# Split weights of an input projection kept in device memory by the first block and loaded by the later ones

## The chip, the cores and the metric

The kernel runs on one core of a Trainium2 chip, as one launch. The metric is device time in microseconds (us), the median of several runs. Lower is better.

## The reference

The program is one layer of a sequence model on x of 2048 tokens by 1024 channels, float32. The normalised input goes through one wide input projection; three groups of heads (a gated DeltaNet, an RWKV-7 and an HGRN2 group, 8 heads of 64 each) work on slices of it, each with a recurrence over time; their outputs go through one output projection and are added to x, and a last RMSNorm follows.

```python
def reference(x, norm_w, w_in, ...):
    for l in range(DEPTH):                      # DEPTH = 1
        h = _rmsnorm(x, norm_w[l])              # (1, 2048, 1024)
        proj = (h @ w_in[l]).astype(F32)        # the input projection
        p_gdn, p_rwkv, p_hgrn = _split(proj, (GDN_PROJ, RWKV_PROJ, HGRN_PROJ))
        y_a = _gdn_branch(p_gdn, ...)
        y_b = _rwkv7_branch(p_rwkv, ...)
        y_c = _hgrn2_branch(p_hgrn, ...)
        y = jnp.concatenate([y_a, y_b, y_c], axis=-1).astype(x.dtype)
        x = x + y @ w_out[l]
    return _rmsnorm(x, final_norm_w)
```

## The kernel before, in words

**Blocks.** The 2048 tokens go through in four blocks of 512 (`TB`, `NT` = 4). For each block, `block` (line 606) loads x, normalises it, transposes it on TensorE and leaves the normalised input in two halves of lower precision, `hhi` and `hlo`, whose sum is the value. Each block then needs the whole input projection: 49 column tiles of 128 columns, each over the 1024 input channels. A tile comes in four parts (`KD // KH`), each of 256 input channels (`KH` = 2 times 128).

**A part of a tile.** The weights are split in two as well. `fetch` (line 499) loads 128 KB of raw weights of `w_in` into a tile `wr` by a DMA on SP's queue; `split` (line 505) makes the high half `wh` by a copy on ScalarE, which rounds to the type fp32r, and the low half `wl` by a subtraction on GpSimd. The part is then six matmuls into one PSUM bank: for each of the two slices of 128 channels wh with hhi, wh with hlo, and wl with hhi. The pool `wp` has `AHEAD` = 4 buffers for wh and for wl each, and `NWR` = 3 for wr (lines 331 to 335). The names in the trace are formed from the part and the tile: wh0hg is the high half of part 0 of tile hg, wl1rv the low half of part 1 of tile rv, mmhg the PSUM bank of tile hg.

**Halves.** Five of the 49 tiles of a block, the first two (wa, rr) and the last three (rg, gg, hg of the last group of heads), are not done over the 512 tokens at once: first the first 256 tokens of each, then the second 256. These take their weights twice and their matmuls have 256 columns; their names end in h0 and h1 (the trace writes mmgg_3h). So a block has 54 tiles in the program, 216 parts.

**Prefetch.** `stream` (line 513) holds the list of parts and gives `more` (line 517): one call splits the oldest raw part, if three are loaded, and then loads the next raw part. `projections` (line 524) calls it nine times ahead and once behind the last matmul of each part (line 604), so four parts lie split and three raw ones are loaded or on their way. The output projection's first half (`first_half`, whose stream is at line 1182) uses the same `stream` and the same buffers for its activations, which it splits in the same way, toward the end of the program.

```python
                for i in range(KD // KH):
                    wh, wl = ahead.pop(0)
                    for j in range(KH):
                        k = KH * i + j
                        mm(po, wh[:, j, :], hhi[:, hs, k, :], start=(k == 0), stop=False)
                        mm(po, wh[:, j, :], hlo[:, hs, k, :], start=False, stop=False)
                        mm(po, wl[:, j, :], hhi[:, hs, k, :], start=False, stop=(k == KD - 1))
...
                    more()
```

**What else runs.** Beside the projection run the groups of heads, as threads of small operations on all engines: `block` and `decays` for a block, and for each of four pairs of heads p the threads `inputs`, `solve`, `chain`, `gates_out`, `outs` and `hgrn` (threads at line 1485). The recurrences are chains of small matmuls with VectorE in between: `S<-pc,S` adds the bank pc to the state S of the DeltaNet, `h_S<-h_S,tot` scales and adds the HGRN2 state, `g_p` is a run of 21 matmuls of 32 by 64. Loads of x (tiles xt, xa) and stores of the finished y tiles go by DMA, on SP's and ScalarE's queues.

**What sets the order.** Two things. `drive` (line 282) takes the next step of a thread by a string of letters, `ORDER` (line 84): this fixes the program. Then `lay_down` (line 269) takes a table for each of the five engines, `LANES` (lines 131 to 250), that says in which order this engine is to work off its instructions, and pins that order. `Lane` (line 253) records each instruction as it is issued, so all instructions carry line 263 in the profile; they are told apart by their tiles. The buffer pools stay as the program has them: which buffer a tile gets is set by the program, and the table of an engine can only move an instruction within what the buffers allow.

**The end.** After the last block, the second half of the output projection runs from line 1506 on (whi, wlo, yt, yh, yl), with the last RMSNorm.

Of the kernel before, what the change touches and what calls it, by code (L numbers as in the profile page):

```python
# [20 lines left out]
D = 1024  # L21
# [4 lines left out]
C = 32  # L26
# [22 lines left out]
def consts():  # L49
# [20 lines left out]
    for i, l in enumerate(LEVELS):  # L70
# [62 lines left out]
        "c-oa%eQ*`k6+ioS-@bjxOY(dnF%ZxtFDCM(5k>7t?JL1BAwY=W7dj4Y92l(QXw^<@Eq~aN5w%!sYqesF(<v6~P(`euFr~FKXjO`WPW_H8MG&Ka"  # L133
        "4T``!{oQl#-rX1NOgovq`*ru;bI$MM-WQ@%=u@ttBV0`<&@n!Z-r}kB8edAEbCw$DAm=GV%pToDTlq6Sm+Gkp{W5e0)#B}BdKHJdug4fQbQs6G"
        "G>4n<eH$&J0kl1|k-tS-xQpJ#T~VH?wn*)m?N0g?FT~h0@T>|mw_&~p`Ujs$Y5e_-&!!i-p4!l}o<`uwhkO>j%u{gn0-~8o%g`2R3O&kSqfzu1"
        "F3}KT9^y&(VjN<sMSca0`6;LI{U*$N9c|{Bc=80#!;ByD82W@8$)gDplNvii&+&9RfEhE$t&t{4HF~LwZsz4wP3w6j-OV>rKlSnkx`bcE^Sh{("
        "e#|#u)az*z&qX#H_&b!NNBA<-rUCJ8<xYB#*Q4*9bOYZ@%eftq@8RuyDqV^3nrR~4K;P#Ux`rO+D`+jNh{}8kA{mMA2arnx?GvO1QJ)sf&__@4"
        "97H+Db!b1v+&|^fG!K<tPOEu|#9u=-Xh#6WI{Hk|s-nEKFC(Td<kLw{Vy+_cS<U@GO5rvGM=M<_H7TOctKdc&_!cnQK1BW=>fL}$XQ9Ryqt@^6"
        "5YNXr(^1o1h)#`PM`cuf6t2sNTE#vZy>mFK=qL{LHb5I-W}lAp+Zeas#@$5I!H^%JI(^{9BvMg-h-efRAD|-RX+PQn==W869jM;R<ZR>xyq(TR"
        "rF&7CPPz*0%FxX~p#yAez#K*T9^HW$zD*DCAfEtUOrSS0Z!Jc7hL0nnHdOBviE9j<N_%+}eZ=QTtm9CPxv0Tf+;@OARft+~-xY<Z>n!@6i2m(3"  # L140
        "PLyw|rR|qGE<$dLkjD<N`Y;gQj4D6Rdr`kVm}@cKT#Nd>#<$Y#INm`N{{jYkI7GgqQFo=dv%%2GQo+1nyInBs5q9;{g<wNJ@Om1!6j6a$$YrJ="
        "Swvn>^KAKM2k<$95w*&8K~dYm`gag@8W^>JC8O~43TWyqe7BA-f*x9Er0BI9RVtzq$M`6?aEyDQZdJoF5YpJz(;;X^Il)5IxFNyDD#OMqWU?DR"
        "^D=)$W{$GS(`}MRC)z$}|3;kGKw}eVIpR>-`#E0?oiT6X9%$=0?}UaUKT%8$=p|GrO|$6_yq`}-HdlZpe}V=#0J$Df<D=kW3-Egs${GZ3&j(h`"
        "sB9CCR#dzLY?_EK$Dj_?w99CsOQKhCW)S`Rh&)4oHSw!lXQDRk;(@OS);;2v>jd$!(8;yd6?%b08)99?KR~1p^EVLfcM(M|W$7opkrwkl@M}EY"
# [148 lines left out]
def kernel_body(ctx, tc, x, w_in, w_ba, w_lora, w_out, fnw, lnw, par, kst, msk, out, T, dbg=None):  # L293
# [45 lines left out]
    with ExitStack() as ph:  # L339
# [173 lines left out]
        def stream(parts):  # L513
# [1100 lines left out]
```

## Time and profile before

| | us |
|---|---|
| median of 3 runs | 2440.32 |
| the three runs | 2442.41, 2440.32, 2426.66 |
| the profiled execution | 2438.88 |
| its span (first to last instruction) | 2436.9 |
| mean granted clock of TensorE in the span | 0.967 |

The profile is of one execution on the chip. The engines are PE (TensorE matmul), PEld (TensorE's weight loads, which overlap PE), DVE (VectorE), ACT (ScalarE), POOL (GpSimd) and SP, which only issues DMAs here. The granted clock (PEclk) is the share of full speed that the throttle gave TensorE. A view of waits names an engine's first instruction after idle time, and with an arrow what ended it; "issue" means that the profile shows nothing that the engine waited for. In names of tiles the numbers of the block and of the group of heads are mostly left out.

### The profile page before, as it was taken

How to read it: one execution, taken by the hardware profiler on the slowest of the kernel's cores; microseconds unless marked ns; L12 is line 12 of the kernel's file. 1: busy time of each engine (PE TensorE's matmuls, PEld its weight loads, DVE VectorE, ACT ScalarE, POOL GpSimd, SP SyncE). 2: the span in 40 equal slices, each digit the busy share in tenths (PEclk: the TensorE clock that was granted, in tenths of full speed). 3: DMA queues.
4: the chain of work that ended last, by engine and by line, in shares of the span. 5: the costliest groups of instructions: out<-in, count | busy, mean ns of one | idle time of the engine just before them, and what ended most of it. 6: DMA issues, size and time to landing. Idle time of an engine off the chain costs nothing.

```text
span 2436.9 us, 88807 instructions
## 1 busy us (share of the span) xinstructions
PE 2233.4 (92%) x38264; PEld 1771.3 (73%) x38264; DVE 1625.5 (67%) x3430; ACT 1024.0 (42%) x2234; POOL 1203.4 (49%) x1641
## 2 busy tenths in 40 slices
PE   6999999989999999899999999888989998899898
PEld 5777676777777777777777778766777777676687
DVE  4867676767676777777676678666675767641354
ACT  5444444445444444454434445444434443422332
POOL 4655455555445555655555455544455644554200
PEclk8999999989999999999999999899999999899999
DMA  3212122221212122222121121212121112446764
GB/s 111 75 53 73 50 69 72 77 79 61 71 46 75 48 75 66 95 65 73 52 70 56 57 77 63 84 54 66 51 67 58 63 61 71 140 143 211 233 214 170
DMA packets 208153, 206.94 MB, mean 85 GB/s; under 512 B 19472, under 2 KB 179600, under 8 KB 207760
## 3 DMA queue, kind: packets, MB, share of 16 engines
q1 hardware_dynamic: 194944, 173.48, 22.3%
q10 hardware_dynamic: 12816, 27.79, 3.3%
q8 instruction: 299, 4.90, 0.8%
q14 instruction: 94, 0.77, 0.1%
HBM read 171.84 MB, written 29.36 MB: 83 GB/s over the span
## 4 chain that ended last, share of the span: by engine, by line
PE 60%; DVE 26%; issue 5%; DMA 3%; POOL 3%; ACT 2%; SPq 0%; ACTq 0%; POOLq 0%; DVEq 0%
PE pa L263 5%; PE mmrk L263 4%; PE pc L263 4%; PE mmgq L263 3%; PE mmgv L263 3%; PE mmhf L263 3%; PE mmhq L263 3%; DVE slv L263 3%; DVE Tf L263 3%; PE mmrr L263 3%; PE uW L263 2%; DVE h_S L263 2%; DMA wry<-ydram 2%; PE mmgk L263 2%; PE g_p L263 2%
## 5 line engine op out<-in xcount | busy, mean ns | idle before, releaser
L263 PEld LDWEIGHTS pc<-S,M 128*128 128x128 f32 x1024 | 144.9, 193 | 48.1 <-DVE S L263 19.1
L263 PE MATMUL pc<-S,M 128*128 128x64 f32 x1024 | 153.9, 273 | 15.5 <-DVE S L263 9.8
L263 POOL TENSOR_TENSOR wly<-wry,why 128x256 fp32r<-128x256 f32 x96 | 70.8, 746 | 91.4 <-ACT why L263 88.0
L263 DVE TENSOR_TENSOR S<-pc,S 128x128 f32<-128x128 f32 x256 | 72.9, 285 | 63.2 <-PE pc L263 61.6
L263 DVE SCALAR_TENSOR_TENSOR h_S<-h_S,tot 128x64 f32<-128x64 f32 x256 | 100.8, 394 | 17.9 <-ACT h_S L263 13.4
L263 DVE TENSOR_TENSOR slv<-Af,Tf 128x15 f32<-128x15 f32 (+7 forms) x240 | 82.4, 343 | 6.1
L263 DVE TENSOR_TENSOR Tf<-Tf,slv 128x15 f32<-128x15 f32 (+7 forms) x240 | 81.5, 340 | 6.3
L263 ACT ACTIVATE why<-wry 128x256 fp32r<-128x256 f32 x96 | 39.4, 416 | 105.4 <-DMA wry<-ydram 53.4
L263 POOL TENSOR_TENSOR D<-gw,cst 128x512 f32<-128x512 f32 x64 | 70.9, 1112 | 23.3 <-DVE M L263 9.2
L263 POOL TENSOR_TENSOR ss<-ss,mhalf 128x1 f32<-128x1 f32 x16 | 8.8, 550 | 131.7 <-DVE ss L263 131.7
L263 PEld LDWEIGHTS h_l<-h_q,h_k 64*32 64x32 f32 x4096 | 41.5, 107 | 29.2 <-DVE h_P L263 12.3
L263 DVE TENSOR_TENSOR h_k<-h_k,tot 128x256 f32<-128x256 f32 x64 | 37.4, 584 | 31.3 <-PE h_l L263 31.3
L263 PE MATMUL h_l<-h_q,h_k 64*32 64x32 f32 x4096 | 48.7, 201 | 7.5 <-DVE h_P L263 5.5
L263 DVE TENSOR_TENSOR M<-MA,D 64x512 f32<-64x512 f32 x64 | 43.9, 686 | 16.1 <-PE MB L263 14.0
L263 PE MATMUL pa<-whi,yl 128*128 128x512 f32 x128 | 50.9, 397 | 2.5 <-DVE yl L263 2.5
L263 PE MATMUL pa<-whi,yh 128*128 128x512 f32 x128 | 50.6, 395 | 0.0
L263 ACT ACTIVATE uW<-uW 128x1024 f32<-128x1024 f32 x32 | 32.8, 1024 | 42.0 <-PE uW L263 42.0
L263 PE MATMUL pa<-wlo,yh 128*128 128x512 f32 x128 | 50.4, 394 | 0.0
L263 POOL TENSOR_TENSOR h_e<-h_k,h_q 128x512 f32<-128x512 f32 (+1 forms) x32 | 37.6, 1175 | 24.5 <-DVE h_q L263 23.9
L263 DVE TENSOR_TENSOR h_q<-h_q,tot 128x256 f32<-128x256 f32 x64 | 39.1, 611 | 15.7 <-PE h_l L263 15.7
L263 DVE COPY_PREDICATED h_P<-mlev,h_l 128x128 f32<-128x128 int32 x128 | 36.6, 294 | 18.3 <-PE h_l L263 18.3
L263 PE MATMUL pa<-hhi,why 128*128 128x512 f32 x112 | 47.4, 423 | 1.1 <-ACT why L263 1.1
(934 smaller groups left out, 8241.1 us busy)
## 6 DMA issues: line engine op xcount, KB each, us to landing
wry<-ydram SPq DMA_DIRECT2D x96, 128.0 KB, 2.9
yt<-ydram SPq DMA_DIRECT2D x16, 768.0 KB, 5.1
xt<-x SPq DMA_DIRECT2D x32, 256.0 KB, 3.1
rdram<-xa SPq DMA_DIRECT2D x32, 256.0 KB, 3.3
out<-xo ACTq DMA_DIRECT2D x16, 512.0 KB, 2.6
ydram<-r_y SPq DMA_DIRECT2D x16, 256.0 KB, 2.8
ydram<-g_y SPq DMA_DIRECT2D x16, 256.0 KB, 2.7
ydram<-h_y SPq DMA_DIRECT2D x16, 256.0 KB, 2.8
```

What stands on the lines that cost most here:

```text
L263: i = f(*a, **k)
```

## The change

`split` writes both halves into one tile `w` of 128 by 2 by 256 (256 KB), and in block 0 SP stores this tile to a buffer `wdram` in device memory: for each whole tile and for the first half of each halved tile, so for 49 tiles times 4 parts. In blocks 1 to 3 no part is fetched raw or split: `reload` loads the tile of 256 KB from `wdram` into one of the four buffers of `w`. `more` then does one thing per call, a reload, as long as the next part comes from `wdram`; so four parts lie ahead in place of four split and three raw ones. The six matmuls of a part and their order stay. The table `LANES` is made anew for all five engines; `ORDER` is the same. `Lane` stands at line 253 in the changed kernel.

| instructions in the program | before | after |
|---|---|---|
| POOL | 1646 | 998 |
| ACT | 2277 | 1629 |
| SP | 1114 | 1310 |
| PE | 22718 | 22718 |
| DVE | 3432 | 3432 |

```diff
     "sync": (
...
-        ">T?MP3Wq-az7M<w^Y{a+-{K("),
...
+        "iS+Mim?W?(MXZe3(C%UweSfL)1H|Odvj"),
...
     NSA, NSO, NRAW, KH, AHEAD, NWR = 6, 2, 9, 2, 4, 3
     NAR, NQK, NKP = 2, 2, 1
     NHF, NHL, BLEAD = 2, 3, 7
+    wdram = dp.tile([w_in.shape[0], KD // KH, 128, 2, KH, 128], F32, name="wdram")
...
-        def split(wr, name):
-
-            wh = wp.tile([128, KH, 128], F32R, name="wh" + name, tag="wh")
-            act(wh, wr, AF.Copy)
-            wl = wp.tile([128, KH, 128], F32R, name="wl" + name, tag="wl")
-            gps.tensor_tensor(wl, wr, wh.bitcast(F32), ALU.subtract)
-            return wh, wl
+        def split(wr, name, keep=None):
+
+            w = wp.tile([128, 2, KH, 128], F32R, name="w" + name, tag="w")
+            act(w[:, 0], wr, AF.Copy)
+            gps.tensor_tensor(w[:, 1], wr, w[:, 0].bitcast(F32), ALU.subtract)
+            if keep is not None:
+                syn.dma_start(keep, w.bitcast(F32))
+            return w[:, 0], w[:, 1]
+
+        def reload(src, name):
+
+            w = wp.tile([128, 2, KH, 128], F32R, name="w" + name, tag="w")
+            syn.dma_start(w.bitcast(F32), src)
+            return w[:, 0], w[:, 1]
 
         def stream(parts):
 
             parts, fetched, ahead = list(parts), [], []
 
             def more():
-                if len(fetched) == NWR or not parts and fetched:
+                ready_ = parts and parts[0][0] is None
+                if fetched and (len(fetched) == NWR or not parts or ready_):
                     ahead.append(split(*fetched.pop(0)))
-                if parts:
-                    fetched.append(fetch(*parts.pop(0)))
+                elif ready_:
+                    _, name, kept = parts.pop(0)
+                    ahead.append(reload(kept, name))
+                    return
+                if parts and parts[0][0] is not None:
+                    src, name, *keep = parts.pop(0)
+                    fetched.append(fetch(src, name) + tuple(keep))
             return more, ahead
...
-            more, ahead = stream([(w_in[ti].rearrange("p (k c) -> p k c", c=128)[:, KH * i:KH * (i + 1)], f"{i}{name}{tb}_{p}" + ("" if half is None else f"h{half}"))
+            more, ahead = stream([(w_in[ti].rearrange("p (k c) -> p k c", c=128)[:, KH * i:KH * (i + 1)] if tb == 0 else None,
+                                   f"{i}{name}{tb}_{p}" + ("" if half is None else f"h{half}"), None if tb == 0 and half == 1 else wdram[ti, i])
                                   for ti, name, tb, p, half in tiles for i in range(KD // KH)])
```

The order of the instructions changes with it. The first place is SP's queue in the middle of block 1, at the tiles gg and hg of the heads p = 1, before the change: each row is the load of a raw part of 128 by 256 values into one of the three wr buffers, with the semaphores that it waits for (a wait for Pool is a wait for a subtraction on GpSimd, a wait for DMAHW one for earlier DMAs).

```order
L263 DMA wr0gg1_1_12232<-w_in 128x256 [waits DMAHW0_49,Pool_49]
L263 DMA wr1gg1_1_12250<-w_in 128x256 [waits DMAHW1_49,Pool_49]
L263 DMA wr2gg1_1_12262<-w_in 128x256 [waits DMAHW2_49,Pool_49]
L263 DMA wr3gg1_1_12289<-w_in 128x256 [waits DMAHW3_49,Pool_49]
L263 DMA wr0hg1_1_12313<-w_in 128x256 [waits DMAHW7_49,DMAHW4_49,Pool_49]
```

After the change the same place of SP's queue reads as follows.

```order
L253 DMA w0gg1_1_11860<-wdram_71 128x512 [waits DMAHW6_49,PE_49]
L253 DMA w1gg1_1_11880<-wdram_71 128x512 [waits DMAHW7_49,PE_49]
L253 DMA w2gg1_1_11888<-wdram_71 128x512 [waits DMAHW4_49,DMAHW0_49,PE_49]
L253 DMA w3gg1_1_11908<-wdram_71 128x512 [waits DMAHW1_49,PE_49]
L253 DMA w0hg1_1_11927<-wdram_71 128x512 [waits DMAHW2_49,PE_49]
```

A load is twice as wide, comes from `wdram`, and waits for PE (the last matmul on the part that had the buffer) where it waited for GpSimd.

The second place is GpSimd's queue in the same block and heads, from the first copy of the tile rawgk's neighbours (rawrk) to the tile rawgq, before the change. The rows wl are the subtractions; D101, D111, r_kt, r_bC, r_kC are operations of the head groups, halr and halg carry the last tokens from one block to the next.

```order
L263 COPY halr_117<-rawrk1_1_11107 128x1
L263 TENSOR_TENSOR wl0gk1_1_11143<-wr0gk1_1_10998,wh0gk1_1_11141 128x256
L263 TENSOR_TENSOR D101_0_11383<-gw1_0_10758,cst_60 128x512
L263 TENSOR_TENSOR D111_0_11385<-gw1_0_10758,cst_60 128x512
L263 TENSOR_TENSOR r_kt1_1_11121<-r_kt1_1_11121,r_k1_1_10132 128x512
L263 COPY gw1_1_12862<-gam_1_8868 128x8x2
L263 TENSOR_TENSOR wl1gk1_1_11186<-wr1gk1_1_11069,wh1gk1_1_11184 128x256
L263 COPY gw1_1_12862<-r_wend1_1_11008 128x8x2
L263 TENSOR_TENSOR wl2gk1_1_11207<-wr2gk1_1_11089,wh2gk1_1_11205 128x256
L263 COPY rawgk1_1_11519<-halg_115 128x3
L263 TENSOR_TENSOR wl3gk1_1_11219<-wr3gk1_1_11145,wh3gk1_1_11217 128x256
```

After the change the same stretch of GpSimd's queue holds:

```order
L253 COPY halr_118<-rawrk1_1_10794 128x1
L253 COPY rawrv1_1_10914<-halr_118 128x1
L253 TENSOR_TENSOR D111_0_11048<-gw1_0_10477,cst_60 128x512
L253 COPY gw1_1_12377<-gam_1_8779 128x8x2
L253 TENSOR_TENSOR r_kt1_1_10808<-r_kt1_1_10808,r_k1_1_9915 128x512
L253 COPY gw1_1_12377<-r_wend1_1_10703 128x8x2
L253 COPY rawgk1_1_11174<-halg_116 128x3
```

The subtractions are gone, and what is left has closed up; D101 stands ahead of the shown rows now.

The third place is PE's queue at the end of block 1, at the halved tiles rg and gg of the heads p = 3 (mmrg1_3h0, mmgg1_3h0), after the change; w2, w3 and w0 are the tiles that a reload fills, and a row with x2 is two matmuls of one form (here the low half's and the next slice's).

```order
L253 MATMUL mmrg1_3h0_15509<-hhi_140,w2rg1_3h0_15480 128x256
L253 MATMUL mmrg1_3h0_15509<-hlo_141,w2rg1_3h0_15480 128x256
L253 MATMUL mmrg1_3h0_15509<-hhi_140,w2rg1_3h0_15480 128x256 x2
L253 MATMUL mmrg1_3h0_15509<-hlo_141,w2rg1_3h0_15480 128x256
L253 MATMUL mmrg1_3h0_15509<-hhi_140,w2rg1_3h0_15480 128x256
L253 MATMUL g_ptv1_3_15513<-cst_60,g_v1_3_15176 128x128 x4
L253 MATMUL mmrg1_3h0_15509<-hhi_140,w3rg1_3h0_15507 128x256
L253 MATMUL mmrg1_3h0_15509<-hlo_141,w3rg1_3h0_15507 128x256
L253 MATMUL mmrg1_3h0_15509<-hhi_140,w3rg1_3h0_15507 128x256 x2
L253 MATMUL mmrg1_3h0_15509<-hlo_141,w3rg1_3h0_15507 128x256
L253 MATMUL mmrg1_3h0_15509<-hhi_140,w3rg1_3h0_15507 128x256
L253 MATMUL mmgg1_3h0_15643<-hhi_140,w0gg1_3h0_15603 128x256
```

Between these parts PE has only the four transposes g_ptv, as before the change; other matmuls near this place (h_po, h_px, not shown) have moved by a few rows.

## Rows read from the trace of the kernel before

**Rows 1.** The page's busy time, share of the span and instructions of each engine.
```profile
PE 2233.4 (92%) x38264; PEld 1771.3 (73%) x38264; DVE 1625.5 (67%) x3430; ACT 1024.0 (42%) x2234; POOL 1203.4 (49%) x1641
```

**Rows 2.** Stretches: us, busy of PE, PEld, DVE, ACT, POOL, granted clock, DMA share, GB/s.
```profile
0.00:61.00 61.00, 41.92 (x298) 33.97 (x298) 27.09 (x63) 33.93 (x85) 25.22 (x55) 0.86 0.35 111
61.00:500.00 439.00, 407.83 (x7296) 317.34 (x7296) 323.60 (x701) 191.43 (x420) 240.98 (x321) 0.98 0.21 68
500.00:2074.00 1574.00, 1456.20 (x27811) 1160.99 (x27810) 1114.06 (x2430) 689.60 (x1524) 826.10 (x1126) 0.97 0.21 65
2074.00:2437.00 363.00, 327.47 (x2864) 259.02 (x2862) 160.76 (x239) 109.05 (x206) 111.15 (x142) 0.96 0.58 185
```

**Rows 3.** PE's waits, 500 to 2074 us: sum in us, number, longest.
```profile
PE g_p L263 <- issue: 12.8, 8, 2.3
PE pxt L263 <- DVE xt L263: 11.2, 4, 4.7
...
PE mmhg L263 <- ACT wh0hg L263: 8.7, 5, 2.3
...
PE mmgg_3h L263 <- issue: 0.5, 1, 0.5
...
PE MA L263 <- DVE r_Lk L263: 0.3, 1, 0.3
...
PE mmrr_0h L263 <- POOL wl0rr_0h L263: 0.2, 1, 0.2
```

**Rows 4.** PE's timeline behind a gap: start, us, instruction, count, idle before.
```profile
728.38 0.53 PE L263 MATMUL g_p<-uW,g_KP 32*32 32x64 f32 x21 [2.33 <-issue]
730.09 0.63 PE L263 MATMUL mmhq<-hlo,wh0hq 128*128 128x512 f32 x1
730.51 0.63 PE L263 MATMUL mmhq<-hhi,wl0hq 128*128 128x512 f32 x1
```

**Rows 5.** PE's timeline in a full run of a whole tile.
```profile
753.83 0.40 PE L263 MATMUL mmrg<-hhi,wh0rg 128*128 128x512 f32 x1
754.06 0.39 PE L263 MATMUL mmrg<-hlo,wh0rg 128*128 128x512 f32 x1
```

**Rows 6.** A split, by tile: least, median and longest ns of 16; when; shapes.
```profile
L263 POOL TENSOR_TENSOR wl1rv<-wr1rv,wh1rv x16: 724/730/1349, 60.3 to 1917.0; 128x256 fp32r<-128x256 f32 x16
...
L263 ACT ACTIVATE wh0gv<-wr0gv x16: 400/417/419, 77.9 to 1941.3; 128x256 fp32r<-128x256 f32 x16
```

**Rows 7.** DMAs: issues with KB and median us to landing; landings of tile xt.
```profile
xa<-rdram ACTq DMA_DIRECT2D x16, 256.0 KB, 3.4
xo<-x ACTq DMA_DIRECT2D x16, 256.0 KB, 3.9
...
DMA to landing us min/median/max: 2.6/3.1/5.5
```

**Rows 8.** PE's timeline at halved tiles of the end of a block.
```profile
994.80 0.28 PE L263 MATMUL mmgg_3h<-hhi,wh0gg_3h 128*128 128x256 f32 x1
994.92 0.28 PE L263 MATMUL mmgg_3h<-hlo,wh0gg_3h 128*128 128x256 f32 x1
...
998.10 0.28 PE L263 MATMUL mmhg_3h<-hhi,wh0hg_3h 128*128 128x256 f32 x1
```

**Rows 9.** DVE's timeline, two steps of the HGRN2 state.
```profile
688.03 0.76 DVE L263 SCALAR_TENSOR_TENSOR h_S<-h_S,tot 128x64 f32<-128x64 f32 x1
...
690.35 0.27 DVE L263 SCALAR_TENSOR_TENSOR h_S<-h_S,tot 128x64 f32<-128x64 f32 x1
```

**Rows 10.** POOL's timeline at the first of these two steps.
```profile
687.52 1.19 POOL L263 TENSOR_TENSOR wl3gk<-wr3gk,wh3gk 128x256 fp32r<-128x256 f32 x1
```

**Rows 11.** The page's groups: busy us, mean ns, idle before and what ended most.
```profile
L263 DVE TENSOR_TENSOR S<-pc,S 128x128 f32<-128x128 f32 x256 | 72.9, 285 | 63.2 <-PE pc L263 61.6
L263 DVE SCALAR_TENSOR_TENSOR h_S<-h_S,tot 128x64 f32<-128x64 f32 x256 | 100.8, 394 | 17.9 <-ACT h_S L263 13.4
```

**Rows 12.** The page's DMA queues: packets, MB, share of 16 engines' span.
```profile
q8 instruction: 299, 4.90, 0.8%
```

More of the change, by code (lines that the diff above doesn't have):

```diff
@@ new lines @@
+        "%dJ<{_4}jAnN#(<y1J^~efPfiYKZ#LSKOJt=2EJl4o*=mZQ(KW7B|y!zK9;<Rtl&qzR8eJN7<v1w2P0UL;M}8p~ty}GPED7YGgKrzC^|)bQ*2q"
+        "DRhKOs8af!G@OUg9zLHQ;UCZ<ew8-zRXC-Y&c;4dDT{NCa1HgRZJdP_%9c%h2mKB$po3ga>oD63wj}8vd<yy`t>CfrKGwbgi??F-bsk4k=qAjb"
+        "f&MP+vYzMjNLX+!U5{}<xAMo-1}q1761CHG#%XjsSI`!!;;yuT`tk7;IOWvD%c)$}+|RQqMR)Q8u&Y0w?&GWIk9;u@J_amH_(E7Pgm!R0nhlRF"
+        "K$}Wy`8w==27I~%xaRRfdJelhD=7a8uhh`fd;^uy!+aif7DUT=8_%RSu|5eaujI|>FX2txNcU1NuA>!H$0typU!ln~nO~%UFQYZUaXLMLcPaWM"
+        "FXgP$$h-I>s^`(ps{BZ2bN(PVI;->3Fu$AkQD@#ymE4Qg!}fXnYZ^@Rc@aIp*MjXFe&@i~m(%aL9sV5)c21&;!A=D=0n74ylar-w`D&*lU*|YL"
@@ new lines @@
+        "wwmgxm6u|#$N77}wG>#gKvqf%_=iA|1`}<(jGp9ksfBv;Cv-ZmfM2^qOXH{qJn#tpmam{cb6+q!h5Ep=)8O;hcp}tQ1FyUb3zFcqj$Ve&R)NPP"
+        "EdxIzXeAWe4}AQDZsFT#CWT<Nj(gIpbPZO{p>t^@e*w>C!0-~9#fSNRtUMEJ)zTR7m4WS5w3mC(XIupY9nj|>XjAF^URYj7W4Vcz(ms9|GxNaH"
+        "BXk@5G9D+NMi<h9@Y4lQ=@=;QRH(2C{3S^#yB1jY@H-f_(DTs5FtC(_2fyS>Se$3Y?on2LTEZiY%2nj})CK6ihIjU&<?(eAeVX1EK1#65aB8E6"
+        "@cb0Kax3K!KPt*D<?(b0&Ea3r&4`orJQ&eC0KWV?&e*}d@x@^HaX8vg>|O$os1v7(4eb(Xo#-$;-VTdiKul~!Q#$V>bJfykr7y?IJgZ!w^!gq&"
+        "zYcqT1ormB+JndmYX2V80LF)4%}VgK8)~Zt?hkk?@<<0_crSNCY(CG2xE}ZhVW)p%<w5Yd4^j9Z?4W!!11By7@~eTd18kLmtv#@NFx1g3(Y}&L"
@@ new lines @@
+    "scalar": (
+        "c-o~_O>^5e5QPEo(~_MgY18RU4?Xn%|C(NU>h#cNCdoLlzD0`Lw+|piQlurP!+}KtyAQi>9~L$yGv1s;M`E_}!R#e96~+dmj_(bI!{2*jjfgcm"
+        "^CUmg@3Z`5K8eFh4TMJCoA$jXg2N6cDa-+H3097h!D5HMM=3E|0<n@DUj^Qdw6ADeV<)xpro~E)#$|z$Gp={$qqOmd40K<8TfnYBE}nZ<^sJbr"
+        "W{?<-RBaMdVy?j>QX{`DW)Fx)y_5m9b&Pij{}X1m@&Md>42}GNT`X2DaMZ4nE!I*-l$tN{h}CcKNa&}tAIv{;VqA&&3RLCO4Wcj2Dz5LimS8O>"
+        "^Nzb7$ds-K>?|KoMk_G+2$ak`$uIcbA-*55|2wnB{4=Z<@Y!P5ugFC6KgwI+tmO@?-rzSUPX&hMj?Y-voqjfd;4NV+Yxr;QwL`RN<UYrY#_SNC"
+        "+ApxGk$cQ9fm^_GMHLj76IRxvwpxe4&5HaeS^=L0c0Gs?GXs_?Btu49L|IFynO0>1Mif!M8miC{t)k5qQ3~RHU@j~8>dwl?3F{538PwJQKU5&c"
+        "dr*|(1ubiR992}&KJRLf#q%JT-^bh<s>)HXs<#DpDU2#xqf%a!hfr-B>sk<584KqmL=mtuqHD&U{Cj4pQ3(~QJE(VvC!7@Z3ch;Ew3>CdqvMMD"
+        "9_X*CSjBvGzKkb8wRU8#d7P1mV`;UArq<HLvwEU-H9oZ(;{R^`WVAuEp?`RDPgG@9@sy=|vLoGIX{<%Y?<QvDIO`ZmX|%c<M6%&}LIg{t);Q4x"
+        "`3jiYXUdpE5wpuo=nT5kNopck#@w*lj-A3q##3tKNCr}NwLb3|ak7r3OYW7OG~&F>zMgnR%sVvgIC`$0<*bsFHn%dZ*@phDDhy*08D7lrt6g%("
+        "z8Jb&$!-xC4ktfo$+BygU9{nhw`VEsP?H#2BYj>S`)od9wBj9+MJ}(iny_XE)?nZ9>e%;npN#!FHIF=JiTPW8Gk*cAL^u4^{2L=`;tisVugUm^"
+        "S{Jb3d6y`YdTulRhMu<PJ)kj$eDy7Ks&8`a@>sIV>Uf4?_dGi_HR#y$PE^*Z>+OO4q`Th&cFG>BHL+&N%IGbc@Qw<~D45?9?&2`CT1(ym8?36Q"
+        "cJPNAhNJG<5xSVha>qwmxI?UW-D7+2!^ij5`d*hFu7~~F$4$)H(U*-@u3NK{9(J_iy07nvZ0@l$U-pKqhS9r0j(sb4b+`W)^)!cmCSo_4nVpHp"
+        "_VRHPmiAS8u(Nx#Ds?a5y2&cpD-4ZuPUBAL2&K4z)&9I^7e2F{_B_&2zV3pJ3?u1u9U@3NjZZ7ijZSpCvmNkjXLNXXwH8zOt*?*&=LRc3Q32oU"
+        "Grq$=b2O#?d4A6;V}CzV_GOlKrn9&>THal>9A@fnU}}zi$N#~m>vis7?nb8VAp6#~<b2xYnY^Ma4D+!A1-qzRd!h5oin(5G&WsM#ex228C+uZ~"
+        "`bmsy-5{C7wUa0A`+Bjxa>Jf8^F77di*Dsdw`3pt<uNsroBsfp`f5x"),
```

190 lines of the change are left out of this document (78 added, 112 removed).

## The prediction

> **What bounds the kernel now.** First the page's busy row [rows 1]: TensorE (PE) works 92% of the span, VectorE (DVE) 67%, GpSimd (POOL) 49%, ScalarE (ACT) 42%. The two engines that the change relieves are the two least busy, so the time they lose is not the time that the kernel gains; that must come out of what PE waits for. Then the busy time by stage [rows 2]. The work divides into the start (0 to 61 us), the rest of the first block (61 to 500), blocks 1 to 3 (500 to 2074) and the end (2074 to 2437). The change takes splits away in blocks 1 to 3 alone. There PE is busy 1456.2 of 1574 us, so 117.8 us idle, at a mean granted clock of 0.97. Third, the list of PE's waits in that stretch [rows 3], by what ended them. The reader is to see three families. Waits ended by DVE: 25 rows from 11.2 down to 0.3, sum 61.7 us in 62 waits, so 1.0 us each. Waits ended by nothing the profile shows (issue): 9 rows from 12.8 to 0.5, sum 33.2. Waits for a split weight, that is for a wh of ACT or a wl of POOL: 13 rows from 8.7 to 0.2, sum 21.5 us in 22 waits. Only the last are what the change removes by its own words. All three are small beside 1456 us of matmuls, which stay: the same products, in the same three terms.
>
> Idle time costs a little more than itself. After the gap of 2.33 us [rows 4] the next matmuls of 512 columns start 0.42 us apart; in a full run they start 0.23 us apart [rows 5]. That is the lower of the clock's two levels (1.2 and 2.4 GHz) for some matmuls behind a gap. A mean of 0.97 over 1574 us is at most 47 us of lost work, 0.4 us for each us of idle; nought is the other end, and since part of the low clock falls into the gaps I take 0.25.
>
> **The change, part by part.**
>
> *Splits that go.* Blocks 1 to 3 have 54 tiles each (49, of which 5 are done as two halves) in 4 parts: 648 parts. Each had an ACT copy of 0.417 us and a POOL subtraction of 0.73 us [rows 6]: 270 us of ACT and 473 us of POOL that run beside PE. On the path stand only PE's 21.5 us for weights. They go: -21.5, bounds 0 (the new wait is as long) and -21.5.
>
> *Loads that take their place.* A reload is 256 KB where a fetch was 128 KB, so 85 MB more in 1574 us: 54 GB/s on top of 65 [rows 2], where the end of the kernel moves 185. It needs a free one of four slots, so it can't be issued before PE has done with the part four places back. Before, four split parts and three raw ones lay ahead. What is queued behind a reload on SP is the next reload, a store of a finished y tile or a load of x; a store that waits for DVE now holds reloads back that have three parts of cover and not seven. Loads of x, of the same size and row length, land 3.1 us after issue at the median, 2.6 to 5.5; at the end of the kernel they take 3.4 and 3.9 [rows 7]. I add 0.6 us for SP's issue and two hand-overs (estimate). A part of a full tile is six matmuls at 0.23 us [rows 5], 1.38 us; four of them 5.5. A slot's own turn is 1.38 + 0.6 + landing, 5.1 us at 3.1, so back-to-back full tiles just hold, up to a landing of 3.5. A part of a half tile is six at 0.12 us, 0.71, and four in a row, with the transpose between them, took 3.3 us in the trace [rows 8]; the turn is 0.71 + 0.6 + 3.1 = 4.4, so about 1.1 us is lost per four. By the new order of PE 48 of the 120 half parts stand that close, 12 turns: 13 us; I take 14. Bounds: 0 (ended by other work between), and at a landing of 3.9 22 us on halves plus 0.4 on the 27 turns of full tiles with nothing between (108 parts in the new order), 11: 33 us.
>
> *DVE beside a quieter POOL.* One step of h_S takes 0.27 us with POOL's operands elsewhere and 0.76 us while a weight subtraction runs on POOL, and ends as it ends [rows 9, 10]: DVE is held until POOL's instruction is over. The mean of 256 such steps is 0.394 [rows 11], 0.12 above the free one, 31% of their time. The splits were 473 of POOL's 826 us in blocks 1 to 3, 57%, so a row of 16 such steps should shrink by 16 x 0.12 x 0.57 = 1.1 us, about one mean DVE wait of PE. Where PE waits for DVE behind such operations the wait can vanish; bounds 0 (the order packs PE differently and waits elsewhere) and -61.7. I take two fifths, -25, because the step that closes PE's recurrence gains nothing: S<-pc,S reads pc from the matmul's bank and its mean of 256 is 0.285 [rows 11].
>
> The Trainium skill, page "SBUF — State Buffer", section "Who interferes with whom", puts this as an exclusive lock: a DVE instruction with both inputs in SBUF and a GpSimd instruction that reads SBUF block each other for a whole instruction, one with a single SBUF input doesn't. The trace agrees at both places (0.27 against 0.76, and 0.285 throughout). By this rule alone all of DVE's family except waits that follow pc and M could go, and the sum would be some 20 us lower than with my two fifths.
>
> *Issue waits.* Left as they are: 0. They fall into runs of tiny matmuls (g_p first). Instructions come by DMA as well, 299 packets of 16 KB in 0.8% of 16 engines' 2437 us [rows 12], 1.04 us each. More traffic could lengthen these, fewer gaps could leave them in cover: bounds -16 and +33.
>
> *Block 0.* It keeps its splits and stores 196 parts of 256 KB, 51 MB, from the queue that also fetches. The store waits for POOL's subtraction, as the next fetch did already (it needs the raw slot which that frees), so SP waits for no one new; a slot is now held until its store has landed, some 3 us, while PE comes to a part later than that. PE, at 407.8 of 439 us, covers it. +5 us for the start and this block, bounds 0 and +15.
>
> *New order.* On PE the rows differ in place, not in number; ACT and POOL lose the splits and close up. I give it no term of its own: what it can win is in the DVE family.
>
> *The sum.* -21.5 + 14 - 25 + 5 = -27.5; a quarter of the 32.5 us of idle less in blocks 1 to 3 for the clock, -8: -35.5. The profiled execution took 2438.9 us (span 2436.9), 1.4 below the median of the runs, 2440.3. 2438.9 - 35.5 = 2403 us.
>
> **Rivals.**
>
> *More goes.* ACT and POOL free, DVE a fifth quicker: the new order leaves PE hardly a DVE wait (-61.7) and a lighter load (+5): (-21.5 - 61.7 + 5) x 1.25 + 5 = -93, 2346 us. For it: mean waits of 1.0 us are within what one chain gains. Against: PE at 92% has to wait somewhere, and startup and the end are untouched.
>
> *Nothing to measure.* PE is the bound, and the weight waits turn into reload waits of the same length; DVE's gain is slack: 2425 to 2450, say 2435. For it: ACT and POOL idle more than half the time [rows 1], and 21.5 us is under 1%.
>
> *Slower: four slots are too few.* One mechanism: landings in the busy stretches beyond the cover. At 4.5 us the 12 half turns lose 2.5 each (30), the 27 full turns 1.0 (27), and 20 more turns with little between 0.5 (10): 67; block 0 with the same landings 10; against -46.5 saved. +30.5 x 1.25 = +38, 2477 us. It decides from a landing of about 4.1 us. For it: a full run asks for 256 KB each 1.38 us, 190 GB/s, and one load of x took 5.5 us. Against: 3.4 and 3.9 us at the kernel's end with 185 GB/s. The Trainium skill, page "DMA: Bandwidth & Descriptors", section "Latency and other measured facts", says that the fixed part of a DMA grows with the load on the memory; the rows agree in direction (3.1 against 3.4 and 3.9), and its upper figure of 2 us more would put the landing at 5 and this rival first.
>
> **How the numbers follow.** Forecast 0.50, more goes 0.16, nothing 0.18, slower 0.16. A measurement of this kernel tells about 1% from no change, 24 us: faster means below 2416, slower above 2464. Of the forecast's half, 0.40 lies below 2416 and 0.10 above. Faster: 0.40 + 0.16 = 0.56. Same: 0.10 + 0.18 and a little of the slower case, 0.29. Slower 0.15. The range leaves out the end of "more goes" and of "slower": 2335 to 2468.
>
> **What would show it.** In the changed kernel's profile: POOL some 500 us and ACT some 270 us less busy; mean of h_S nearer 0.33 us; PE's waits for wh and wl gone from blocks 1 to 3, and waits on DMA of w tiles of some 14 us, nearly all on the half tiles; landings of w from wdram of 3.1 to 3.4 us; DVE-ended waits under 40 us; PE's busy time nearly the same. It is wrong if reload landings are above 4 us, if full tiles wait for them, if issue waits double, or if PE's idle time in blocks 1 to 3 has not fallen by 25 us or more.

## The result, and the profile after

The changed kernel takes 2367.81 us (median of 4 runs, 2352.40 to 2368.77), the kernel before beside it 2435.23 (4 runs): ratio 0.9702, 95% interval 0.9676 to 0.9727. It is faster by 3.0%, where 1.5% was forecast (2403 us). Inside the range, on the forecast side, and twice the size.

First the page's busy row of the changed kernel.

```profile
PE 2204.5 (93%) x38264; PEld 1757.6 (74%) x38264; DVE 1482.6 (63%) x3430; ACT 794.9 (34%) x1586; POOL 677.1 (29%) x993
```

Against [rows 1] GpSimd works 526 us less and ScalarE 229 less (500 and 270 were forecast). Two other engines have the same instructions as before and yet work less: VectorE by 143 us, PE by 29. These two carry the result.

The same four stretches of time as in [rows 2], for the changed kernel (us, busy of PE, PEld, DVE, ACT, POOL, granted clock, DMA share, GB/s):

```profile
0.00:61.00 61.00, 38.05 (x285) 30.69 (x285) 26.49 (x62) 32.36 (x81) 21.41 (x50) 0.89 0.47 153
61.00:500.00 439.00, 404.05 (x7246) 310.97 (x7246) 306.81 (x647) 183.86 (x404) 230.27 (x313) 0.99 0.51 169
500.00:2074.00 1574.00, 1491.82 (x29166) 1201.04 (x29165) 1030.16 (x2566) 497.11 (x956) 346.45 (x528) 0.98 0.44 128
2074.00:2367.00 293.00, 270.61 (x1572) 214.92 (x1570) 119.10 (x157) 81.58 (x147) 78.95 (x104) 0.97 0.63 200
```

In the third stretch PE does 29166 matmuls where it did 27811, and idles 82 us where it idled 118. Data moves at 128 GB/s in place of 65, 9 more than the 54 reckoned for the reloads (the last stores of block 0 and the beginning of the end now fall into the stretch).

PE's waits in that stretch, to be laid beside [rows 3] (us in total, times, longest):

```profile
PE pX L253 <- DVE Bn L253: 12.5, 11, 3.0
PE g_p L253 <- issue: 8.5, 6, 2.0
PE pxt L253 <- DVE xt L253: 7.9, 4, 3.0
...
PE mmhg_3h L253 <- DMA w1hg_3h<-wdram: 1.3, 1, 1.3
...
PE mmrg L253 <- DMA w2rg<-wdram: 0.9, 1, 0.9
...
PE mmhg_3h L253 <- DMA w3hg_3h<-wdram: 0.7, 1, 0.7
...
PE mmgg_3h L253 <- DMA w3gg_3h<-wdram: 0.6, 1, 0.6
...
PE mmrg_3h L253 <- DMA w3rg_3h<-wdram: 0.5, 1, 0.5
...
PE mmhg L253 <- DMA w3hg<-wdram: 0.4, 1, 0.4
```

Waits for ACT's and POOL's weights are left only in the last tiles of block 0, which now reach into this stretch. Waits for reloads are small, 4.8 us in eight rows, and six of the eight lie on halved tiles (two of 0.2 us are not shown). Counted between the blocks' own bounds (first matmul of block 1 to the last projection matmul: 523.6 to 2103.5 us before, 553.6 to 2046.8 after), PE's idle time fell from 124.6 to 65.3 us: VectorE-ended waits from 67.9 to 27.2, waits for weights from 23.5 to none, reloads 0 to 4.8, issue 31.9 to 28.5.

VectorE's two groups of [rows 11], after:

```profile
L253 DVE TENSOR_TENSOR S<-pc,S 128x128 f32<-128x128 f32 x256 | 73.4, 287 | 82.8 <-PE pc L253 79.8
...
L253 DVE SCALAR_TENSOR_TENSOR h_S<-h_S,tot 128x64 f32<-128x64 f32 x256 | 83.1, 325 | 14.9 <-ACT h_S L253 10.4
```

The step that reads PE's bank is unchanged (285 and 287 ns); the step with both operands in SBUF went from 394 to 325 ns. Half of the 648 reloads land within 2.7 us of their issue. Below are rows by DMA issue, and the landing of tile w0hi (its 12 reloads and 4 stores together):

```profile
xt<-x SPq DMA_DIRECT2D x32, 256.0 KB, 3.8
...
w0rk<-wdram SPq DMA_DIRECT2D x12, 256.0 KB, 2.7
...
w0hi<-wdram SPq DMA_DIRECT2D x12, 256.0 KB, 2.8
...
w3hg_3h<-wdram SPq DMA_DIRECT2D x6, 256.0 KB, 4.1
...
DMA to landing us min/median/max: 2.1/2.7/4.7
```

The loads of x took 3.1 us in [rows 7] and take 3.8 here (4.2 in the run order_kept below), so a load that is the same before and after lands later than it did. The reloads of the last halved tiles have medians of 2.7 to 4.1 us by tile.

### The profile page after: what moved, and what is told of

Same layout as the page of the kernel before. It is cut to its first block, busy times and chain, and to the rows that moved or that the text cites. A ratio compares the mean times of both kernels' runs of the same rounds, so it can differ in the third digit from the quotient of the medians.

```text
span 2367.0 us, 86943 instructions
## 1 busy us (share of the span) xinstructions
PE 2204.5 (93%) x38264; PEld 1757.6 (74%) x38264; DVE 1482.6 (63%) x3430; ACT 794.9 (34%) x1586; POOL 677.1 (29%) x993
## 4 chain that ended last, share of the span: by engine, by line
PE 72%; DVE 14%; issue 5%; DMA 4%; ACT 3%; POOL 2%; SPq 0%; ACTq 0%; POOLq 0%; DVEq 0%
PE pa L253 6%; PE pc L253 5%; PE mmrk L253 4%; PE mmhq L253 4%; PE mmgv L253 4%; PE mmgq L253 4%; PE mmrv L253 4%; PE mmgk L253 4%; PE mmhf L253 3%; PE mmrr L253 3%; PE uW L253 3%; DMA wry<-ydram 2%; PE mmhi L253 2%; PE r_po L253 2%; DVE Tf L253 2%
## 5 line engine op out<-in xcount | busy, mean ns | idle before, releaser
L253 PEld LDWEIGHTS pc<-S,M 128*128 128x128 f32 x1024 | 145.1, 191 | 28.6 <-DVE S L253 6.7
L253 POOL TENSOR_TENSOR wy<-wry,wy 128x256 fp32r<-128x256 f32 x96 | 71.8, 759 | 92.1 <-ACT wy L253 90.6
L253 POOL TENSOR_TENSOR D<-gw,cst 128x512 f32<-128x512 f32 x64 | 71.4, 1116 | 83.7 <-DVE rawhg L253 34.1
L253 DVE SCALAR_TENSOR_TENSOR h_S<-h_S,tot 128x64 f32<-128x64 f32 x256 | 83.1, 325 | 14.9 <-ACT h_S L253 10.4
L253 PE MATMUL pa<-hhi,wy 128*128 128x512 f32 x224 | 74.3, 412 | 3.1 <-ACT wy L253 2.5
L253 ACT ACTIVATE wy<-wry 128x256 fp32r<-128x256 f32 x96 | 38.7, 416 | 113.7 <-DMA wry<-ydram 77.0
L253 DVE TENSOR_TENSOR Tf<-Tf,slv 128x15 f32<-128x15 f32 (+7 forms) x240 | 63.8, 266 | 6.4
L253 DVE TENSOR_TENSOR slv<-Af,Tf 128x15 f32<-128x15 f32 (+7 forms) x240 | 60.5, 252 | 6.1
L253 POOL TENSOR_TENSOR g_n<-g_n,mhalf 128x8 f32<-128x8 f32 x16 | 26.6, 1660 | 110.4 <-DVE g_n L253 110.4
L253 DVE TENSOR_TENSOR h_k<-h_k,tot 128x256 f32<-128x256 f32 x64 | 32.6, 510 | 32.3 <-PE h_l L253 32.0
L253 PEld LDWEIGHTS pa<-hhi,wy 128*128 128x128 f32 x224 | 41.6, 195 | 12.6 <-ACT wy L253 3.0
```

Of the source, the lines that this page charges most:

```text
L253: i = f(*a, **k)
```

## The experiments

Theory A: GpSimd's reads of SBUF hold VectorE, and their end is most of the gain. Theory B: the new tables made what the forecast missed. Theory C: it was the removed waits for weights. All kernels stand against the kernel before in the same session; a ratio of 0.970 is the changed kernel.

**order_kept: the change without new tables.** The diff to the changed kernel is the five tables alone.

> The changed program with the old tables: PE and VectorE work in exactly the order of the kernel before, ScalarE and GpSimd in that order without the splits of blocks 1 to 3, SP with each reload and each store in the place of a fetch. Theory A (relief: quiet GpSimd frees VectorE, and weight waits are gone) expects most of the gain without new tables: 2375 to 2395 us, VectorE-ended waits of PE in blocks 1 to 3 falling from 68 to 40 us or less. Theory B (the new tables made the gain beyond the forecast) expects 2400 to 2415, about what the prediction named, with VectorE-ended waits near 55 us.

2361.75 us, ratio 0.9681 (0.9655 to 0.9707): the whole gain, with the old order. Theory B falls. It is also the cleanest pair to read, since PE does the same 27738 matmuls in blocks 1 to 3. First the kernel before, then order_kept, blocks 1 to 3 between their own bounds (columns as above):

```profile
523.60:2103.50 1579.90, 1455.32 (x27738) 1159.94 (x27738) 1122.70 (x2448) 689.35 (x1523) 827.00 (x1123) 0.97 0.21 66
```

```profile
523.00:2026.00 1503.00, 1426.68 (x27738) 1148.88 (x27738) 983.05 (x2449) 463.94 (x879) 312.77 (x477) 0.98 0.44 126
```

76.9 us shorter: 48.3 us less idle, and 28.6 us less busy for the same work. VectorE-ended waits fell from 67.9 to 23.7 us, weights 23.5 to none, reloads rose to 16.1, issue 33.6. So 44.2 of the 48.3 us come from waits that VectorE ended; what the weights no longer take is mostly taken by the reloads. Three rows of VectorE's, two of the kernel before and one of order_kept:

```profile
PE pX L263 <- DVE Bn L263: 15.3, 7, 5.9
...
PE pc L263 <- DVE S L263: 5.2, 8, 1.3
```

```profile
PE pX L249 <- DVE Bn L249: 10.1, 4, 6.2
```

**after_again, order_kept_again.** The two once more side by side, five rounds.

> The changed kernel once more, beside order_kept on one chip in five rounds, to tell whether the new tables add or cost anything. New tables worth nothing: 2360 to 2370 us, within 6 us of the run beside it. New tables a loss (they put 20 us of PE's idle time into block 0): 8 us or more above it.

> order_kept once more. New tables worth nothing: 2357 to 2368 us, within 6 us of the changed kernel. New tables a loss: 8 us or more below it.

2366.55 (ratio 0.9705, 0.9684 to 0.9726) and 2359.16 (0.9692, 0.9665 to 0.9719). 7.4 us apart, between the two cases named, with intervals that overlap: the new tables bring nothing, and whether they cost a few us can't be told.

**few_stores.** Only the four parts of tile wa are stored, and reloaded for all tiles, so it leaves out the weights of all other tiles in blocks 1 to 3.

```diff
-... None if tb == 0 and half == 1 else wdram[ti, i])
+... None if tb == 0 and (half == 1 or name != "wa") else wdram[0, i])
```

> Stores only the four parts of tile wa in block 0 and reloads these same four for every tile, so the weights of all other tiles in blocks 1 to 3 are not the reference's; 192 stores of 256 KB are gone, all else as in the changed kernel. If the stores cost block 0 its 21 us of extra idle time (by holding a slot till they land, or by standing between fetches on SP), the time falls by 20 to 35 us to 2335 to 2348, and waits for weights in block 0 fall from 28 to about 16 us. If the new tables had moved that idle time into block 0 (VectorE and issue waits there), it stays at 2360 to 2370.

2365.13, ratio 0.9687 (0.9666 to 0.9708): 192 stores cost next to nothing. Weight waits of the first block stay at 28.9 us in its trace. What lengthened block 0 of the changed kernel (15 to 523.6 us before, 14.9 to 553.6 after) is the new tables: in order_kept it takes 507.6 us with all its stores.

**pool_sub, pool_set.** The changed kernel with idle work on GpSimd for each of the 648 reloads.

```diff
+    spare = cp.tile([128, KH, 128], F32R, name="spare")
...
             syn.dma_start(w.bitcast(F32), src)
+            gps.tensor_tensor(spare, cst[:, 0:256].rearrange("p (k c) -> p k c", c=128), cst[:, 256:512].rearrange("p (k c) -> p k c", c=128), ALU.subtract)
```

That is pool_sub; pool_set has, in the place of the last line, twice

```diff
+            gps.memset(spare.rearrange("p k c -> p (k c)"), 0.0)
```

> The changed kernel with one idle subtraction of 128x256 on GpSimd per reload (648, both inputs from constants in SBUF, result used by nobody). GpSimd gets back its 473 us, PE waits for none of them directly. Theory A (VectorE is held while GpSimd reads SBUF): VectorE busy rises by 100 us or more, mean of h_S from 0.325 to about 0.39 us, VectorE-ended waits in blocks 1 to 3 from 27 to 50 us or more, time 2400 to 2425. Theory B (order): under 2380.

> The same with two memsets of 128x256 per reload (about 0.62 us, 400 us in all) in place of the subtraction: GpSimd as busy but reading nothing. Theory A: VectorE's durations stay as in the changed kernel (h_S 0.32 to 0.34 us) and the time stays within 10 us of it, 2365 to 2378. If it is the time that GpSimd's own results come late that costs, and not a held VectorE, it is as slow as with the subtractions, 2400 or more.

pool_sub 2497.16 (1.0227, 1.0197 to 1.0256), pool_set 2373.16 (0.9739, 0.9711 to 0.9768). 648 subtractions that nobody waits for cost 129 us, more than the change had won; 410 us of memsets cost 5 (9 by the ratios, whose intervals overlap). So it is not that GpSimd is busy, it is that it reads. The subtractions' cost went beyond what was expected; they stood in clusters of up to 14 in a table made for a quiet GpSimd, which led to the next run.

**kept_sub, kept_act, kept_copy.** order_kept with the idle subtraction at exactly the places where the kernel before had its own; then an idle ScalarE copy at the old places of the copies; then a GpSimd copy with one input in the subtraction's place.

The line of kept_sub is that of pool_sub; those of kept_act and kept_copy are

```diff
+            act(spare, cst[:, 0:256].rearrange("p (k c) -> p k c", c=128), AF.Copy)
...
+            gps.tensor_copy(spare, cst[:, 0:256].rearrange("p (k c) -> p k c", c=128))
```

> order_kept with an idle subtraction of 128x256 on GpSimd (both inputs constants in SBUF, result used by nobody) at each of the 648 places where the kernel before had a subtraction. Against the kernel before, only the splits' results are no longer waited for and ScalarE's copies are gone; against order_kept, only GpSimd's reads are back. Theory A (GpSimd's reads hold VectorE, and that is most of the gain): 2405 to 2435, VectorE busy back above 1600 us, PE's VectorE-ended waits in blocks 1 to 3 from 24 to 50 us or more. Theory C (the removed waits for weights are most of the gain, and the 130 us of the other subtraction run came from its clusters): under 2385.

> order_kept with an idle copy of 128x256 on ScalarE at each of the 648 places where the kernel before had a copy (270 us of ScalarE back, nothing waits for the results). Theory A gives ScalarE no share: 2355 to 2370. If ScalarE's relief mattered (results of ScalarE late for PE or VectorE), 2375 or more.

> order_kept with an idle copy of 128x256 on GpSimd (one input, from SBUF) at each of the 648 places where kept_sub has a subtraction. Theory A (any read of SBUF by GpSimd holds VectorE for its length): the copies take about 0.4 us where the subtractions took 0.84, so about half of the subtractions' 93 us comes back: 2395 to 2420. If only GpSimd instructions with two inputs hold VectorE: 2358 to 2375.

kept_sub 2454.74 (1.0092, 1.0057 to 1.0126), kept_act 2363.58 (0.9704, 0.9688 to 0.9720), kept_copy 2374.03 (0.9739, 0.9716 to 0.9761). The idle work in the page's groups of kept_sub, kept_act, kept_copy and, for comparison, pool_set (busy us, mean ns):

```profile
L256 POOL TENSOR_TENSOR spare<-cst 128x256 fp32r<-128x256 f32 x648 | 543.4, 839 | 25.3
```

```profile
L255 ACT ACTIVATE spare<-cst 128x256 fp32r<-128x256 f32 x648 | 266.9, 412 | 8.2
```

```profile
L256 POOL COPY spare<-cst 128x256 f32<-128x256 f32 x648 | 325.3, 502 | 19.8
```

```profile
L262 POOL MEMSET spare<- 128x256 f32 x1296 | 409.6, 316 | 56.9
```

Against order_kept the reads cost 93 us (100 by the ratios), ScalarE's 267 us nothing that can be told (2, or 6 by the ratios), and the one-input copies 12 (14). Theory C falls as the main cause: with the reads back and the waits for weights still gone, the kernel is slower than before. Nor is it that GpSimd's own results come late: VectorE waits for GpSimd 37.4 us in kept_sub's blocks 1 to 3, 35.7 in order_kept, 31.2 before. The expectation for kept_copy, half the price, was wrong, and the other one, nothing, nearly right. Beside a running copy the step h_q<-h_q,tot takes 0.61 us (median of the 18 that overlap one), beside a subtraction 0.90 (of 25), free 0.42 in both runs: a copy holds VectorE too, but 0.19 and not 0.48 us, and being shorter it meets fewer of its steps. Where GpSimd's reads return in kept_sub one chain pays most (PE's waits in blocks 1 to 3):

```profile
PE pX L256 <- DVE Bn L256: 47.9, 10, 9.0
PE g_p L256 <- issue: 13.3, 7, 2.8
PE mmhg_3h L256 <- DMA w0hg_3h<-wdram: 9.2, 3, 4.5
```

Before, this wait for Bn had 15.3 us in blocks 1 to 3, in order_kept 10.1 (rows above). kept_sub's blocks 1 to 3 in one row, to be laid beside the two of order_kept's section:

```profile
528.40:2121.70 1593.30, 1454.28 (x27738) 1162.73 (x27738) 1137.81 (x2449) 464.02 (x879) 841.94 (x1124) 0.96 0.41 119
```

VectorE is back at 1138 us for its 2449 instructions. The idle subtractions wait for nothing, so they run at other moments than the old ones, and 93 us might overprice the reads: VectorE-ended waits are 91.2 us where they were 67.9 before. The three kernels after this go into that.

**kept_tied.** kept_sub, with the subtraction reading the reloaded tile.

```diff
+            gps.tensor_tensor(spare, w[:, 0].bitcast(F32), w[:, 1].bitcast(F32), ALU.subtract)
```

> kept_sub with the 648 subtractions tied to the reloaded tile (both inputs are the two halves of w, result used by nobody), so each starts only once its part has landed, in GpSimd's old order, as the old ones started once ScalarE's copy was done. Against the kernel before, GpSimd then reads as much and nearly at the same times, and only PE's waits for weights have become waits for reloads. If GpSimd's reads are the whole gain, it takes as long as the kernel before, 2425 to 2445. If the removed waits for weights are worth something of their own, 2395 to 2425. If kept_sub's 2455 was right for the price of the reads and not a matter of when they ran, 2445 or more.

2520.98 (1.0331, 1.0291 to 1.0370), the slowest of all. A reload is issued when PE frees a slot, so GpSimd's queue now follows PE, and VectorE waits for GpSimd (107.9 us in blocks 1 to 3): VectorE-ended waits of PE are 140.7 us there. It says what such a tie costs, and nothing on how the gain divides.

**both_ways, both_set.** In blocks 1 to 3 the raw load, ScalarE's copy and GpSimd's subtraction run as in the kernel before, in its order on all engines, into a spare tile t of one buffer; PE reads the reloaded w. both_set has a memset of t in the subtraction's place.

```diff
...
+                    else:
+                        t = wp.tile([128, KH, 128], F32R, name="t" + name, tag="t", bufs=1)
+                        act(t, wr, AF.Copy)
+                        gps.tensor_tensor(t, wr, t.bitcast(F32), ALU.subtract)
+                        ahead.append(reload(kept, name))
```

> The kernel before with its raw loads, ScalarE copies and GpSimd subtractions all kept in blocks 1 to 3, in its own order on every engine, but their results go to a spare tile, and PE reads the reloaded w. So the splits run when they ran before; only PE's wait for their results has become a wait for the reload (and 170 MB more of loads). If GpSimd's reads carry the whole gain, the time is that of the kernel before, 2425 to 2450. If PE's waits for weights are worth something of their own, 2395 to 2425.

> both_ways with one memset of 128x256 (0.31 us, into the same spare tile, so it waits for ScalarE's copy as the subtraction did) in place of each of the 648 subtractions: nothing differs but that GpSimd does not read. Its distance to both_ways is the price of the reads in the place where the kernel before had them. If the reads are the gain: 2355 to 2385, 60 us or more below both_ways. If the order in which they ran made most of kept_sub's loss: less than 40 us below.

both_ways 2512.54 (1.0298, 1.0281 to 1.0316), both_set 2411.90 (0.9890, 0.9863 to 0.9916). They are 101 us apart, but more differs than the reads. A memset doesn't read the raw tile, so in both_set the raw loads on SP no longer wait for GpSimd, and the reloads stand behind them in that queue: SP waited 589 us for GpSimd in both_ways' blocks 1 to 3 and 5 in both_set, where it waited 265 for ScalarE. PE idles 67.5 us less there, 47.8 of it in waits for reloads (90.8 to 43.0) and 21.5 in waits that VectorE ended (34.1 to 12.6). What the pair does show is VectorE's busy time; the first row is both_ways, the second both_set:

```profile
PE 2271.4 (90%) x38264; PEld 1784.6 (71%) x38264; DVE 1623.7 (64%) x3430; ACT 1026.4 (41%) x2234; POOL 1204.9 (48%) x1641
```

```profile
PE 2226.7 (93%) x38264; PEld 1763.4 (73%) x38264; DVE 1492.6 (62%) x3430; ACT 1023.7 (43%) x2234; POOL 871.0 (36%) x1641
```

131 us more on the same 3430 instructions, and the row of both_ways is that of the kernel before on DVE, ACT and POOL. both_ways itself doesn't show what the removed waits were worth: with raw loads and reloads on one SP queue, PE waits 90.8 us for reloads in its blocks 1 to 3 where the kernel before waited 23.5 for weights. So the price of the reads in the place where the kernel before had them has no clean measurement; nearest to it is the pair of the kernel before and order_kept, with its 44.2 us of VectorE-ended waits.

**kept_five, kept_back, kept_back_five.** What makes PE wait for reloads. Five buffers (to make room, the constants' matrix of ones becomes one column that is read 128 times); the 39 stores of y of blocks 1 to 3 moved behind the next five reloads in SP's table; both.

```diff
-            w = wp.tile([128, 2, KH, 128], F32R, name="w" + name, tag="w")
+            w = wp.tile([128, 2, KH, 128], F32R, name="w" + name, tag="w", bufs=5)
```

> order_kept with five buffers for w in place of four; the order of every engine unchanged (512 bytes of constants, the matrix of ones, become one column read 128 times, to make room). If reload waits (16 us of PE in blocks 1 to 3, nearly all on halved tiles) come from the slot's turn, as the prediction has it, they fall to 5 us or less and the time by 10 to 18 us, to 2343 to 2352. If they come from what stands ahead on SP's queue, they stay, at 2355 to 2365.

> order_kept with SP's stores of finished y tiles in blocks 1 to 3 (39 of them) moved behind the next five reloads; nothing else moves, four buffers. If reload waits come from a store that waits for VectorE at the head of SP's queue (10 us or more of the 16 in order_kept's trace have such a store right ahead), PE's waits for w fall from 16 to 6 us or less and the time by 5 to 15 us, to 2347 to 2358. If they come from the turn of the slots, nothing changes.

> The same with five buffers for w. If both causes add, PE's waits for w fall to 2 us or less and the time to 2340 to 2352. If only the queue mattered, it equals kept_back.

kept_five 2356.54 (0.9674, 0.9646 to 0.9701), kept_back 2404.21 (0.9863, 0.9834 to 0.9891), kept_back_five 2370.94 (0.9723, 0.9700 to 0.9746). Waits for reloads in blocks 1 to 3: 16.1 us in order_kept, 13.3 with five buffers, 14.1 with the stores moved, 6.5 with both. Neither cause alone, then. The longest wait of order_kept, on SP's queue and on PE:

```profile
1485.50 0.32 SPq L249 DMA_DIRECT2D ydram<-h_y  x1
1485.87 0.43 SPq L249 DMA_DIRECT2D xt<-x  x1
1486.39 0.40 SPq L249 DMA_DIRECT2D w0hg_3h<-wdram  x1
```

```profile
1490.02 0.55 PE L249 MATMUL mmhg_3h<-hhi,w0hg_3h 128*128 128x256 f32 x1 [4.20 <-DMA w0hg_3h<-wdram]
```

A store that waits for VectorE stands ahead, then a load of x, then the reload; it lands 3.5 us after its issue. With the store moved the load of x and the slot's turn take its place. And moving the stores was a bad bargain: a y buffer now stays taken till PE has gone through five more parts. ScalarE and GpSimd waited 70.5 us for stores of y in blocks 1 to 3 (4.5 in order_kept), and PE's waits ended by VectorE and ScalarE in blocks 1 to 3 rose from 25.7 to 60.2 us. The order of SP's queue was already a compromise, which the expectation of 5 to 15 us faster had not seen.

The fastest medians are kept_five and order_kept, both below the kernel before beyond doubt; that they are below the changed kernel is not shown, since their intervals overlap its own.

## Why the prediction was right or wrong

- **Where the gain comes from: right.** PE's idle time in blocks 1 to 3, not the 755 us that GpSimd and ScalarE lose. kept_act and pool_set show the second half of that: work on either engine that VectorE doesn't feel costs 2 and 5 us by the medians, which can't be told from nothing.
- **Splits that go, -21.5: right as a term, and partly taken back by its partner.** The waits for weights went to none. In the old order the reloads brought 16.1 us back, in the new one 4.8; +14 had been taken. Their mechanism was half right: most lie on the halved tiles (13.3 of the 16.1), but five buffers took away 2.8 us only. The sentence on a store at the head of SP's queue named the other half and was not priced.
- **VectorE beside a quieter GpSimd, -25: the step that failed first.** "I take two fifths, -25, because the step that closes PE's recurrence gains nothing." It gained nothing (285 to 287 ns), but PE's waits behind it were 5.2 of 67.9 us to begin with (row pc of the kernel before, above), and fell to 1.8 in order_kept even so; other chains had the waits. Three fifths went, -40.7 (order_kept -44.2). The bounds held. The rule of the Trainium skill, page "SBUF — State Buffer", section "Who interferes with whom", had been put to one side as a variant of the sum; its result, 20 us lower, is the one that the trace bears out. The prediction's "one with a single SBUF input doesn't" left out a condition that the section has: it names `tensor_scalar` among the operations that, in a faster mode, can take the ports shared with GpSimd even with one input. The trace agrees: xt<-xt,xm, one SBUF tensor, takes 0.48 us free and 0.95 beside a subtraction (medians in kept_sub). The whole group, least, median and longest ns, in kept_sub and in order_kept:

```profile
L256 DVE TENSOR_SCALAR xt<-xt,xm x32: 451/940/1483, 6.7 to 1580.3; 128x512 f32<-128x512 f32 x32
```

```profile
L249 DVE TENSOR_SCALAR xt<-xt,xm x32: 452/483/1470, 6.9 to 1514.8; 128x512 f32<-128x512 f32 x32
```

- **The clock, -8: the step that failed second.** "Since part of the low clock falls into the gaps I take 0.25" for each us of idle less. Busy time for the same 27738 matmuls fell by 28.6 us for 48.3 us of idle, 0.59 each; from kept_sub to order_kept by 27.6 for 62.7, 0.44 (kept_sub's row of blocks 1 to 3 stands above). Over the span the mean granted clock rose from 0.967 to 0.977, and to 0.980 in order_kept. The upper bound taken, 0.4, was a mean over all idle time at the kernel's own clock; what a change removes can be dearer than the mean. With 0.6 and three fifths of VectorE's family the same sum gives (-21.5 + 14 - 41) x 1.6 + 5 = -73, 2366 us; that it comes so near is partly luck, since the terms for reloads and block 0 were off too.
- **Block 0, +5: wrong in cause.** The stores cost nothing that can be told (few_stores). In the changed kernel start and block 0 have 21.3 us more idle time than before, 2.6 in order_kept, so the new tables put it there. Against order_kept the changed kernel's trace is 30.6 us longer in start and block 0 and 17.3 shorter behind.
- **New order, no term: right.** **Issue waits, 0: right** (31.9 to 28.5 and 33.6 us).
- **The whole in traces.** Span 2436.9 to 2367.0, -69.9: idle -41.0 (blocks 1 to 3 -59.3, start and block 0 +21.3, end -3.0), busy -28.9.
- **Rivals.** "More goes" (2346) had the right cause; 27 of VectorE's 68 us remain. "Nothing to measure" fell with VectorE's slack. "Four slots are too few" asked for landings of 4.1 us; they were 2.7 at the median, at 128 GB/s, though 3.2 on the last halved tiles and up to 6.0. The Trainium skill, page "DMA: Bandwidth & Descriptors", section "Latency and other measured facts", has the fixed part grow with the load on the memory; the trace agrees in direction where like stands beside like: loads of x went from 3.1 to 3.8 us (4.2 in order_kept) as the traffic doubled. What was wrong is the prediction's step from loads of x to reloads, which land sooner than these do.

What stays open is how much the removed waits for weights would bring with GpSimd's reads unchanged. kept_sub and both_ways put it at less than nothing, but each added waits for reloads of its own, and kept_sub's reads ran at other moments than the old ones.

## What to carry to other kernels

Before pricing a split, a cast or a subtraction on GpSimd by who waits for its result, look at what it does to VectorE while it runs: here 648 subtractions of 0.84 us cost 93 us in kept_sub, though nothing waited for their results, and two memsets for each in pool_set cost nothing that can be told. Work that can be made once and read back by DMA is cheap if its loads don't stand behind stores that wait for another engine. And a us of PE's idle time was worth about 1.5 us here, so a forecast made from waits alone comes out too small.

## What the runs showed of the hardware that was not expected

- VectorE is held by GpSimd's reads and hardly by its writes: over 648 places, two-input subtractions (0.84 us each) added 153 us to VectorE's busy time (1488.2 to 1641.6) and 93 to the kernel; one-input copies (0.50 us) 37 and 12; two memsets of 0.32 us, on the changed kernel, 3 and 5 (the last within the noise).
- One-input VectorE operations of SBUF to SBUF are held as well (xt above), where a reduction of 128x512 is not: hss<-h_o takes 0.68 us beside a subtraction and 0.69 free in kept_sub.
- 63 GB/s more traffic in blocks 1 to 3 hardly changed PE's issue waits (31.9 us before, 28.5 and 33.6 after). It did lengthen transfers that are the same before and after: loads of x from 3.1 to 3.8 us at the median, 4.2 in order_kept. The reloads of the same 256 KB landed in 2.7.
